# First feed-forward of a hybrid decoder layer: state-space tables built in smaller steps, modulation sums held in their place, fewer table stores

## The chip, the cores and the metric

The kernel runs on one core of a Trainium2 chip. The metric is the device time of one execution in microseconds (us); a run of the kernel before takes 1685.62 us (median of three, 1685.13 to 1685.9). The engines are named as in the profile: PE multiplies matrices (PEld loads its weights), DVE is the vector engine, ACT the scalar engine, POOL is GpSimd, and SP is the engine whose queue issues most of the transfers (DMA).

## The reference, cut to what matters

One decoder layer on a 1024 x 1024 activation, all in 32-bit floats: a gated feed-forward, a mixer of a short convolution and a diagonal state-space model (S5), a second gated feed-forward, a final norm. Shift, scale and gate of each part come from the condition vector.

```python
mod = c_act @ w_mod[l] + b_mod[l]                 # 9 vectors of 1024
h = modulate(rms_norm(x, ffn1_norm[l]), sh1, sc1)
x = x + 0.5 * g1 * swiglu(h, w_gate, w_up, w_down)        # first feed-forward
h = modulate(rms_norm(x, mix_norm[l]), sh2, sc2)
proj = h @ w_in[l]
...
lam_bar = jnp.exp(lam * dt)                       # per group (32) and state (64)
b_bar = ((lam_bar - 1) / lam)[..., None] * b
bu = jnp.einsum('gpc,bsgc->bsgp', b_bar, u)
_, states = lax.associative_scan(combine, (lam_bar, bu), axis=1)
y = jnp.einsum('gcp,bsgp->bsgc', c, states).real + d_skip * u
...
x = x + 0.5 * g3 * swiglu(h2, w_gate, w_up, w_down)       # second feed-forward
```

## The kernel before, in words

Every large product is made of 128 x 512 tiles from operands that are split in a high and a low part; three matmuls (high by high, high by low, low by high) make one product, which the text calls a triple (`mm3`). After each triple a counter (`Clock.tick`) advances, and after every `period` triples one step of a side program (`clock.side`) is recorded. So work for other engines is laid between the matmuls in units of triples. A scheduler then orders each engine's instructions by when their inputs should be there, so an instruction may stand in its engine's queue well before the place at which it was recorded, unless `V.follow` ties it behind another one.

The first feed-forward is `fa0` to `fa10`, eleven groups of 256 hidden columns, and then `fad` and `fald`, its down projection. Groups 1 to 10 use a product with seven multiplications instead of eight (`seven`): seven weight tiles `w`, each for a gate (`g`) and an up (`u`) half of four triples, added up in the PSUM banks A, B and C, in the order B, C, B, C, B, A, B. DVE reads the second C, the third B, the A and the last B and adds them to copies that ACT took earlier (`fa5gu`, `fa5gc`, `fa5gt` and so on). Each weight tile comes as a `raw` tile by DMA; ACT rounds it to the high part, DVE subtracts it to get the low part (both rows are called `w<-raw`), and between two uses of one raw tile POOL starts a DMA that adds another block to it. Four `w` tiles and three raw tiles exist. Sums of the results go to DRAM (`kept`).

Beside the groups a side program (`side1`) works off three things: the left factors of the seven products, then the base of the state-space tables (`ssm_base`), and then eight batches (`ssm_batch`), one for each four of the 32 state groups, with the 24 modulation sums between them.

A batch loads its parameters `prm`, and DVE makes `bb` (the scaled input matrix), `cl` (an output table, with `clt` as its second term), `bl` (an input table, with `blt`) and the rotors `rot` and `rott`. PE then makes `kp` (the kernel of the short Toeplitz matrix) and `tp` (`bl` transposed). ACT copies these to `kc` and `mi`, DVE adds the skip term to the diagonal of `kc`, and the tables go to DRAM: `mo_d`, `co_d`, `si_d`, `mi_d` and the Toeplitz matrices `mk_d`. These rows share four buffers (`bt`). The mixer loads the tables again later.

A modulation sum (`wm`) is one DVE instruction over a 128 x 1024 weight block that a DMA of 512 KB fetches into one of two buffers; the fetch after it waits until the sum has freed the buffer. Before the change, one sum stands after the input table and three after the PE work of each of batches 2 to 7, and nothing ties them to that place.

The line numbers are of little help, since one helper (L113) records nearly every instruction; the rows are found by the names of their tiles.

Of the kernel before, what the change touches and what calls it, by code (L numbers as in the profile page):

```python
# [21 lines left out]
P = 128  # L22
# [9 lines left out]
CH = 16  # L32
# [199 lines left out]
def hymba_layer(ctx: ExitStack, tc, x_d, xt_d, wm1_d, wmod_d, gu1_d, gs1_d, ds10_d, ds11_d, wl1_d, win_d, wout_d, glu_d, gu2_d, gs2_d, wd2_d, ds20_d, ds21_d, ds22_d, wl2_d, cols_d, cond_d, lam_d, bc_d, out_d):  # L232
# [775 lines left out]

    cact_d = scratch.tile([P, 1024], F32, name="cact_d")
    SP.dma_start(cact_d[:], cact[:])  # L1010
    mk_d = scratch.tile([NB, P, GB * P], F32, name="mk_d")
    mi_d = scratch.tile([NB, P, GB * P], F32, name="mi_d")
    mo_d = scratch.tile([NB, P, GB * P], F32, name="mo_d")
    co_d = scratch.tile([NB, P, GB * P], F32, name="co_d")
# [25 lines left out]
    def ssm_base(sb, sb1):  # L1040
# [127 lines left out]
            yield  # L1168
        zero = sb1.tile([CH, 112], F32, name="zero")
        V.memset(zero[:], 0.0)  # L1170
        mk4 = mk_d[:].rearrange("b p (g c) -> p b g c", g=GB)
        for t in range(1, TAU):
            for b in range(NB):
                SP.dma_start(
                    mk4[t * CH : (t + 1) * CH, b, :, 0 : t * CH],
                    zero[:, 0 : t * CH].unsqueeze(1).to_broadcast([CH, GB, t * CH]),
                )
            yield
        ssm.update(q=qq, tabs=tabs, base=baset, step=step, lam=lam)

    def ssm_batch(b):
        bp = bps[0]
        gs = slice(b * GB, (b + 1) * GB)
        prm = bp.tile([P, 4, GB, CH], F32, tag="prm", name=f"prm{b}")
        SP.dma_start(prm[:], bc_d[b])
        bb = bp.tile([P, 2, GB, CH], F32, tag="bb", name=f"bb{b}")
        q = tuple(ssm["q"][:, i, gs].unsqueeze(2).to_broadcast([P, GB, CH]) for i in range(2))
        cmul(bp, bb[:], prm[:, 0:2], q, [GB, CH], f"bb{b}")
        p1, p2, e1, e2 = ssm["tabs"]

        def bt(name):
            return bp.tile([P, 576], F32, tag="bt", name=name, bufs=4)

        def comb(dst, n, lam, src, op, nm):

            t = bt(nm)[:, : GB * n * CH].rearrange("p (g n c) -> p g n c", g=GB, n=n)
            la = [a[:, 0:n, gs].rearrange("p n g -> p g n").unsqueeze(3).to_broadcast([P, GB, n, CH]) for a in lam]
            sc = [a.unsqueeze(2).to_broadcast([P, GB, n, CH]) for a in src]
            V.tensor_tensor(out=dst, in0=la[0], in1=sc[0], op=ALU.mult)
            V.tensor_tensor(out=t, in0=la[1], in1=sc[1], op=ALU.mult)  # L1200
            yield
            V.tensor_tensor(out=dst, in0=dst, in1=t, op=op)

        cl = bt(f"cl{b}")
        cl4 = cl[:].rearrange("p (g n c) -> p g n c", g=GB, n=9)
        yield from comb(cl4, 9, (p1, p2), (prm[:, 2], prm[:, 3]), ALU.add, f"clt{b}")
        SP.dma_start(mo_d[b].rearrange("p (g m) -> p g m", g=GB), cl4[:, :, 1:9, :].rearrange("p g n c -> p g (n c)"))
        bl = bt(f"bl{b}")
        bl4 = bl[:, :512].rearrange("p (g n c) -> p g n c", g=GB, n=8)
        yield from comb(bl4, 8, (e1, e2), (bb[:, 0], bb[:, 1]), ALU.add, f"blt{b}")  # L1210
        if b >= 2:
            yield from gate1()

        def v3(a):
            return a[:, :512].rearrange("p (g m i) -> p g m i", g=GB, m=8)

        bs = [a[:, gs, :].unsqueeze(2).to_broadcast([P, GB, 8, 16]) for a in ssm["base"]]
        st = [ssm["step"][:, i, :, gs].rearrange("p m g -> p g m").unsqueeze(3).to_broadcast([P, GB, 8, 16]) for i in range(2)]

        def rotors():  # L1220

            r, t = bt(f"rot{b}"), bt(f"rott{b}")
            V.tensor_tensor(out=v3(r), in0=st[0], in1=bs[0], op=ALU.mult)
            V.tensor_tensor(out=v3(t), in0=st[1], in1=bs[1], op=ALU.mult)
            yield
            V.tensor_tensor(out=r[:, :512], in0=r[:, :512], in1=t[:, :512], op=ALU.add)
            A.activation(t[64:128, :512], r[64:128, :512], AF.Copy, scale=-1.0)
            for half in (slice(0, 64), slice(64, 128)):
                SP.dma_start(co_d[b, half], r[0:64, :512])
            SP.dma_start(si_d[b, 0:64], r[64:128, :512])  # L1230
            SP.dma_start(si_d[b, 64:128], t[64:128, :512])

        yield from rotors()
        yield

        kp = sm([CH, 512], f"kp{b}")
        for g in range(GB):
            T.matmul(
                kp[:, g * P : (g + 1) * P], lhsT=bl4[:, g, 7, :], rhs=cl4[:, g, 0:8, :].rearrange("p n c -> p (n c)"), start=True, stop=True
            )  # L1240
        tp = sm([P, 512], f"tp{b}")
        for g in range(GB):
            T.transpose(tp[:, g * P : (g + 1) * P], bl[:, g * P : (g + 1) * P], ident[:])
        if b >= 2:
            yield from gate1()
            yield from gate1()
            yield from gate1()
        kc = bt(f"kc{b}")
        kc3 = kc[:CH, :512].rearrange("p (g m) -> p g m", g=GB)
        A.copy(kc[:CH, :512], kp[:])  # L1250
        for g in range(GB):
# [3 lines left out]
        mk3 = mk_d[b].rearrange("p (g m) -> p g m", g=GB)  # L1255
        for t in range(TAU):
            SP.dma_start(mk3[t * CH : (t + 1) * CH, :, t * CH :], kc3[:, :, : P - t * CH])
        mi = bt(f"mi{b}")
        A.copy(mi[:, :512], tp[:])
# [39 lines left out]
    def side1():  # L1299
        yield from combos1()  # L1300
        clock.period = 4.5
        sb = side_open.enter_context(tc.tile_pool(name="sb", bufs=1, side="right"))
        with tc.tile_pool(name="sb1", bufs=1, side="right") as sb1:
            yield from ssm_base(sb, sb1)
        clock.period = BATCH_PERIOD
        bps.append(side_open.enter_context(tc.tile_pool(name="bp", bufs=1, side="right")))
        mod_home.pool = side_open.enter_context(tc.tile_pool(name="wmp", bufs=1, side="right"))
        share[0] = MODS[1]
        for _ in range(2):
            mod_fetch(mod_home)  # L1310
        for b in range(NB):
            yield from ssm_batch(b)

    def side2(home, n):

# [16 lines left out]
            norm_into(act2, h, n2[h], 1, "h2")  # L1332

    movs["B"] = es1.enter_context(tc.tile_pool(name="movB1", bufs=12))
    BATCH_PERIOD = 5.5
    first_open = ExitStack()

    def first_opened():
# [528 lines left out]
```

## Time and profile before

| | us |
|---|---|
| median of three runs | 1685.62 |
| the profiled execution | 1691.33 |
| its span, first to last instruction | 1689.6 |
| PE busy | 1656.7 |
| DVE busy | 1080.9 |
| ACT busy | 685.9 |

The profiled execution is one run with the profiler on, and 5.7 us longer than the median; 1.7 us of its time lie outside the span. PE is busy in nearly all of it. A PE that is busy is not one at its full rate: a row of 12 matmuls that follows another one starts 2.72 us after it at the full rate, and whatever makes this distance longer is lost time.

### The profile page before, as it was taken

The numbers are of one execution on the slowest core, as the hardware profiler recorded it, in microseconds if no ns is written. First come the engines' busy times: TensorE is split into PE (matmuls) and PEld (weight loads), VectorE is DVE, ScalarE is ACT, GpSimd is POOL, SyncE is SP. The second block draws the span as 40 slices with busy tenths as digits, with TensorE's granted clock in tenths as the row PEclk, the third lists the DMA queues.
The fourth block names the chain that finished last, engine by engine and source line by source line (L and its number), as shares of the span: only waits on it lengthen the run. The fifth ranks groups of instructions, "written<-read, shape, count | busy, mean of one in ns | idle before, by whom it ended". The sixth has DMA issues, their size and how long they took to land.

```text
span 1689.6 us, 20672 instructions
## 1 busy us (share of the span) xinstructions
PE 1656.7 (98%) x7509; PEld 1364.8 (81%) x7509; DVE 1080.9 (64%) x1608; ACT 685.9 (41%) x1011; POOL 173.4 (10%) x211
## 2 busy tenths in 40 slices
PE   8999989999999999999999999999999999999998
PEld 5888878878888888787878778888888888888887
DVE  7984777777567758635656847856555555344576
ACT  6654333343465431332214416434444444322345
POOL 2010000001001102100000121001000111000104
PEclk9999999999999999999999999999999999999999
DMA  9467987987898767145653333557887777889832
GB/s 350 138 162 183 264 250 205 266 250 208 256 317 230 181 213 273 38 112 161 200 152 117 97 103 138 137 137 215 228 239 216 211 224 225 271 276 314 245 77 100
DMA packets 128840, 337.06 MB, mean 199 GB/s; under 512 B 22369, under 2 KB 37985, under 8 KB 127714
## 3 DMA queue, kind: packets, MB, share of 16 engines
q1 hardware_dynamic: 112034, 275.96, 47.2%
q0 software_dynamic: 16704, 59.78, 20.3%
q8 instruction: 59, 0.97, 0.2%
q14 instruction: 43, 0.35, 0.1%
HBM read 253.37 MB, written 73.92 MB: 194 GB/s over the span
## 4 chain that ended last, share of the span: by engine, by line
PE 73%; DVE 7%; DMA 5%; issue 1%; SPq 1%; ACT 0%; POOL 0%; DVEq 0%; POOLq 0%; ACTq 0%
PE fald L113 4%; PE wo L113 3%; PE fbd_1B L113 3%; PE fbd_0B L113 3%; PE fad_0B L113 3%; PE fad_1B L113 3%; PE b L113 2%; PE c L113 2%; PE u L113 2%; PE v L113 2%; DMA wm<-in_wmod 2%; PE fbd_1C L113 1%; PE fbd_0C L113 1%; PE fb0u L113 1%; PE fb0d L113 1%
## 5 line engine op out<-in xcount | busy, mean ns | idle before, releaser
L113 DVE TENSOR_TENSOR w<-raw,w 128x1024 fp32r<-128x1024 f32 (+1 forms) x247 | 298.7, 1211 | 264.3 <-ACT w L113 259.9
L113 ACT CAST w<-raw 128x1024 fp32r<-128x1024 f32 (+1 forms) x247 | 256.2, 1039 | 310.5 <-DMA raw<-in_ds 75.6
L175 POOL DMA_DIRECT2D raw<-in_gs x80 | 70.6, 883 | 740.5 <-DVE w L113 461.7
L113 DVE CUSTOM_DVE_ANT_0 wm<-wm,cact 128x1024 f32<-128x1024 f32 x56 | 76.1, 1373 | 36.3 <-DMA wm<-in_wmod 36.1
L175 POOL DMA_DIRECT2D raw<-in_ds x36 | 31.5, 876 | 311.9 <-DVE w L113 177.6
L113 PE MATMUL p<-h,w 128*128 128x512 f32 x192 | 48.7, 401 | 2.3 <-ACT h L113 1.5
L113 PE MATMUL wo<-oa,w 128*128 128x512 f32 x192 | 47.0, 400 | 2.7 <-ACT w L113 2.6
L113 PE MATMUL wo<-ob,w 128*128 128x512 f32 x192 | 45.6, 392 | 1.1 <-ACT ob L113 0.6
L113 PE MATMUL c<-h,w 128*128 128x512 f32 x192 | 46.1, 393 | 0.0
L113 PE MATMUL v<-h,w 128*128 128x512 f32 x192 | 46.0, 393 | 0.0
L113 PEld LDWEIGHTS wo<-oa,w 128*128 128x128 f32 x192 | 36.7, 193 | 11.4 <-ACT w L113 3.0
L113 PE MATMUL u<-h,w 128*128 128x512 f32 x192 | 45.5, 396 | 0.2 <-DVE h L113 0.2
L113 PE MATMUL b<-h,w 128*128 128x512 f32 x192 | 45.1, 392 | 0.0
L113 PEld LDWEIGHTS p<-h,w 128*128 128x128 f32 x192 | 35.1, 189 | 10.6 <-ACT h L113 2.0
L113 PEld LDWEIGHTS wo<-ob,w 128*128 128x128 f32 x192 | 35.7, 188 | 9.2 <-ACT ob L113 1.0
L113 PEld LDWEIGHTS u<-h,w 128*128 128x128 f32 x192 | 36.2, 190 | 8.3 <-DVE h L113 0.6
L113 PEld LDWEIGHTS b<-h,w 128*128 128x128 f32 x192 | 35.7, 188 | 7.2
L113 PEld LDWEIGHTS c<-h,w 128*128 128x128 f32 x192 | 35.7, 189 | 7.0
L113 PEld LDWEIGHTS v<-h,w 128*128 128x128 f32 x192 | 35.5, 188 | 7.0
L113 DVE TENSOR_TENSOR X<-co,X 128x512 f32<-128x512 f32 x8 | 5.5, 693 | 36.1 <-DMA swx<-X 28.1
L113 PE MATMUL fb0u<-h,w 128*128 128x512 f32 x96 | 23.8, 391 | 0.0
L113 PE MATMUL fb0g<-h,w 128*128 128x512 f32 x96 | 23.2, 389 | 0.0
(1554 smaller groups left out, 3882.9 us busy)
## 6 DMA issues: line engine op xcount, KB each, us to landing
raw<-in_gs SPq DMA_DIRECT2D x80, 512.0 KB, 4.8
raw<-in_gs POOLq DMA_DIRECT2D x80, 512.0 KB, 6.5
wm<-in_wmod SPq DMA_DIRECT2D x56, 512.0 KB, 7.2
raw<-in_ds SPq DMA_DIRECT2D x32, 512.0 KB, 5.8
raw<-in_ds POOLq DMA_DIRECT2D x32, 512.0 KB, 7.5
mw<-in_wm SPq DMA_DIRECT2D x8, 1024.0 KB, 8.3
raw<-in_win SPq DMA_DIRECT2D x16, 512.0 KB, 4.4
xb<-in_xt SPq DMA_DIRECT2D x8, 512.0 KB, 9.4
```

The lines of the kernel that those rows point to most:

```text
L113: r = getattr(self.engine, name)(*args, **kw)
L175: self.G.dma_start(out=r, in_=src, accum_op=ALU.add)
```

## The change

Five things are changed in the batches and around them.

- The steps are finer: a batch is cut into 13 pieces instead of five, and one step is recorded every 2.3 triples instead of every 5.5.
- After pieces 1, 5 and 9 of every batch one modulation sum is recorded (three to a batch, 24 in all, as before), and `pools["mixed"] = False` makes each sum follow the DVE instruction that was recorded just ahead of it.
- `kp` and `tp` come after the rotors' last addition; the rotors' copy and stores come behind them.
- The parameters of a batch are loaded during the batch before it.
- A Toeplitz row in DRAM has 256 columns, of which the last 128 take what sticks out, so that one store writes all eight shifted copies of a group's kernel: four stores to a batch instead of eight, and seven stores of zeros instead of 56. The mixer's load of `mk` then reads four rows of 512 bytes in a partition instead of one of 2 KB.

```diff
-    mk_d = scratch.tile([NB, P, GB * P], F32, name="mk_d")
+    mk_row = NB * GB * 2 * P
+    mk_all = scratch.tile([P * mk_row + P], F32, name="mk_d")
+    mk_d = mk_all[: P * mk_row].rearrange("(p b g m) -> b p g m", p=P, b=NB, g=GB)[:, :, :, :P]
+    mk_steps = mk_all[:].rearrange("(t r) -> t r", t=TAU)[:, : CH * mk_row].rearrange("t (c b g m) -> b c t g m", c=CH, b=NB, g=GB)[:, :, :, :, :P]
...
         for t in range(1, TAU):
-            for b in range(NB):
-                SP.dma_start(
-                    mk4[t * CH : (t + 1) * CH, b, :, 0 : t * CH],
...
+            SP.dma_start(
+                mk4[t * CH : (t + 1) * CH, :, 0 : t * CH],
...
     def ssm_batch(b):
...
-        prm = bp.tile([P, 4, GB, CH], F32, tag="prm", name=f"prm{b}")
-        SP.dma_start(prm[:], bc_d[b])
+        prm = ssm["prm"]
...
+        if b + 1 < NB:
+            prm_load(b + 1)
...
-        if b >= 2:
-            yield from gate1()
...
-        if b >= 2:
-            yield from gate1()
-            yield from gate1()
-            yield from gate1()
+        A.activation(t[64:128, :512], r[64:128, :512], AF.Copy, scale=-1.0)
...
-        for t in range(TAU):
-            SP.dma_start(mk3[t * CH : (t + 1) * CH, :, t * CH :], kc3[:, :, : P - t * CH])
...
+        for g in range(GB):
+            SP.dma_start(mk_steps[b][:, :, g, :], kc3[:, g, :].unsqueeze(1).to_broadcast([CH, TAU, P]))
...
+        prm_load(0)
         for _ in range(2):
             mod_fetch(mod_home)
+        yield
+        pools["mixed"] = False
         for b in range(NB):
-            yield from ssm_batch(b)
+            for i, _ in enumerate(ssm_batch(b)):
+                yield
+                if i % 4 == 1:
+                    yield from gate1()
...
-    BATCH_PERIOD = 5.5
+    BATCH_PERIOD = 2.3
```

DVE's queue around the start of `fa4`'s second C and of the first weight tiles of `fa5`, before (the row `ISA wm` is a sum, the short row `ISA gate` or `ISA scl` reads its result):

```order
L113 TENSOR_TENSOR w_1788<-raw_1641,w_1788 128x1024
L113 ISA wm_2_1_2408,gate<-wm_2_1_2408,cact 128x1024
L113 ISA gate 128x1
L113 ISA wm_3_0_2545,gate<-wm_3_0_2545,cact 128x1024
L113 ISA gate 128x1
L113 TENSOR_TENSOR w_1854<-raw_1474,w_1854 128x1024
L113 ISA wm_3_1_2638,gate<-wm_3_1_2638,cact 128x1024
L113 ISA gate 128x1
L113 TENSOR_TENSOR fa4gu_1814<-fa4gu_1814,fa4gC 128x512
L113 TENSOR_TENSOR gate<-gate,cols 128x8
L113 ISA wm_0_0_2659,scl<-wm_0_0_2659,cact 128x1024
```

And the same place of it now:

```order
L113 TENSOR_TENSOR w_1746<-raw_1634,w_1746 128x1024
L113 TENSOR_TENSOR w_1801<-raw_1474,w_1801 128x1024
L113 TENSOR_TENSOR fa4gu_1765<-fa4gu_1765,fa4gC 128x512
L113 ISA wm_0_0_1782,gate<-wm_0_0_1782,cact 128x1024
L113 ISA gate 128x1
L113 TENSOR_TENSOR fa4uu_1799<-fa4uu_1799,fa4uC 128x512
L113 SCALAR_TENSOR_TENSOR fa4Y<-fa4uu_1799,fa4gu_1765 128x512
L113 TENSOR_TENSOR w_1842<-raw_1713,w_1842 128x1024
```

Before, nine sums stand ahead of or among these rows; now three do, and from here to `w_1926`, the tile of `fa5`'s first C, there is none.

SP's queue at the end of `fa4`, before:

```order
L113 DMA raw_1857<-in_gs 128x1024
L113 DMA wm_0_1_2693<-in_wmod 128x1024
L113 DMA wm_1_0_2836<-in_wmod 128x1024
L113 DMA wm_1_1_2925<-in_wmod 128x1024
L113 DMA wm_2_0_2956<-in_wmod 128x1024
L113 DMA wm_2_1_2977<-in_wmod 128x1024
L113 DMA mk_d<-kc_1965 16x512
L113 DMA mk_d<-kc_1965 64x1x112
L113 DMA mk_d<-kc_1965 64x1x96
```

And now:

```order
L113 DMA raw_1804<-in_gs 128x1024
L113 DMA wm_2_0_1945<-in_wmod 128x1024
L113 DMA kept4X<-fa4X 128x1024
L113 DMA raw_1929<-in_gs 128x1024
L113 DMA mk_d<-kc_1976 16x8x128 x2
L113 DMA kept4Y<-fa4Y 128x1024
L113 DMA kept4Z<-fa4Z 128x1024
L113 DMA mk_d<-kc_1976 16x8x128
L113 DMA kept4W<-fa4W 128x1024
```

Five fetches in a row, each waiting for a sum, have become single ones with weight loads and stores between them.

DVE's queue from the second batch's input table to the first addition that PE's second `kp` of the program stands behind, now:

```order
L113 TENSOR_TENSOR w_2083<-raw_1929,w_2083 128x1024
L113 ISA wm_2_0_1945,gate<-wm_2_0_1945,cact 128x1024
L113 ISA gate 128x1
L113 TENSOR_TENSOR bl_2095<-bl_2095,blt_2096 128x512
L113 TENSOR_TENSOR rot_2139<-rs,rt_1405 128x512
L113 TENSOR_TENSOR rott_2140<-rs,rt_1406 128x512
L113 TENSOR_TENSOR rot_2139<-rot_2139,rott_2140 128x512
L113 TENSOR_TENSOR w_2128<-raw_1749,w_2128 128x1024
L113 TENSOR_TENSOR fa5gu_2108<-fa5gu_2108,fa5gC 128x512
```

On PE this `kp` now stands in the third B of `fa5`, behind the second C that the last row reads; before, it stood in the first C of `fa5`, and on DVE the end of `bl` came after `fa4Z`.

## Rows read from the trace of the kernel before

**Rows 1.** The page's first part: busy time, share of the span, instructions.

```profile
PE 1656.7 (98%) x7509; PEld 1364.8 (81%) x7509; DVE 1080.9 (64%) x1608; ACT 685.9 (41%) x1011; POOL 173.4 (10%) x211
```

**Rows 2.** Stretches: length, busy PE, PEld, DVE, ACT, POOL (instructions), PE's clock, DMA share, GB/s.

```profile
230.00:270.00 40.00, 35.00 (x160) 28.04 (x159) 31.92 (x58) 13.32 (x20) 2.66 (x3) 1.00 0.82 242
350.00:390.00 40.00, 38.81 (x176) 31.41 (x175) 33.49 (x59) 15.94 (x22) 4.43 (x5) 1.00 0.87 220
390.00:430.00 40.00, 40.00 (x183) 32.81 (x183) 27.00 (x42) 15.47 (x21) 3.62 (x5) 1.00 0.77 205
```

**Rows 3.** PE in order of time: start, length, engine, instruction.

```profile
190.41 2.88 PE L113 MATMUL fa4gB<-h,w 128*128 128x512 f32 x12
193.13 2.88 PE L113 MATMUL fa4uB<-h,w 128*128 128x512 f32 x12
...
266.98 2.88 PE L113 MATMUL fa5uA<-h,w 128*128 128x512 f32 x12
...
274.00 2.88 PE L113 MATMUL fa5uB<-h,w 128*128 128x512 f32 x12
...
358.56 2.88 PE L113 MATMUL fa8gB<-h,w 128*128 128x512 f32 x12
```

**Rows 4.** Waits of PE from 60 to 480 us: total, times, longest.

```profile
PE kp L113 <- DVE bl L113: 3.3, 1, 3.3
PE fa5gC L113 <- DVE w L113: 1.7, 1, 1.7
PE fa7gB L113 <- DVE fa7gc L113: 1.2, 1, 1.2
PE fa6gB L113 <- DVE fa6gc L113: 0.5, 1, 0.5
```

**Rows 5.** In order of time, 230 to 246 us, with idle time before and its releaser.

```profile
231.14 1.23 DVE L113 CUSTOM_DVE_ANT_0 wm<-wm,cact 128x1024 f32<-128x1024 f32 x1 [1.98 <-DMA wm<-in_wmod]
...
233.28 1.21 DVE L113 CUSTOM_DVE_ANT_0 wm<-wm,cact 128x1024 f32<-128x1024 f32 x1
...
236.57 1.21 DVE L113 TENSOR_TENSOR w<-raw,w 128x1024 fp32r<-128x1024 f32 x1
...
237.83 2.56 PE L113 MATMUL fa5gC<-h1S,w 128*128 128x512 f32 x10 [1.68 <-DVE w L113]
...
244.93 0.67 DVE L113 TENSOR_TENSOR bl<-bl,blt 128x512 f32<-128x512 f32 x1
...
245.75 1.03 PE L113 MATMUL kp<-cl,bl 128*16 128x128 f32 x8 [3.32 <-DVE bl L113]
```

**Rows 6.** DVE's groups by shape, 190 to 440 us: busy, mean ns, idle before.

```profile
L113 DVE TENSOR_TENSOR w<-raw,w 128x1024 fp32r<-128x1024 f32 x44 | 53.7, 1220 | 24.8 <-ACT w L113 24.7
L113 DVE CUSTOM_DVE_ANT_0 wm<-wm,cact 128x1024 f32<-128x1024 f32 x21 | 25.6, 1220 | 18.9 <-DMA wm<-in_wmod 18.8
L113 DVE TENSOR_TENSOR cl<-tab,prm 128x576 f32<-128x576 f32 x7 | 5.3, 755 | 0.4 <-issue 0.3
...
L113 DVE TENSOR_TENSOR blt<-tab,bb 128x512 f32<-128x512 f32 x7 | 4.8, 684 | 4.3 <-DMA mk_d<-kc 4.3
...
L113 DVE SCALAR_TENSOR_TENSOR kc<-ident,lam,kc 16x16 f32<-16x16 f32 x28 | 4.6, 217 | 2.0 <-ACT kc L113 2.0
```

**Rows 7.** The tile `wm`, 160 to 360 us: its fetches from issue to landing.

```profile
DMA to landing us min/median/max: 3.9/6.7/9.8
```

**Rows 8.** SP's queue in order of time, 205 to 250 us: start, length, transfers.

```profile
215.48 17.25 SPq L113 DMA_DIRECT2D wm<-in_wmod  x5
...
233.21 4.82 SPq L113 DMA_DIRECT2D mk_d<-kc  x8
```

**Rows 9.** Transfers by line: count, KB each, median us from issue to landing.

```profile
mk<-mk_d SPq DMA_DIRECT2D x8, 256.0 KB, 4.0
...
ub<-u_d SPq DMA_DIRECT2D x8, 256.0 KB, 4.9
```

**Rows 10.** Waits of PE in the mixer, 690 to 1080 us.

```profile
PE yy L113 <- DVE co L113: 4.3, 3, 2.6
```

More of the change, by code (lines that the diff above doesn't have):

```diff
@@ L1170, in ssm_base, with prm_load @@
         V.memset(zero[:], 0.0)
-        mk4 = mk_d[:].rearrange("b p (g c) -> p b g c", g=GB)
+        mk4 = mk_all[: P * mk_row].rearrange("(p q m) -> p q m", p=P, q=NB * GB)
         for t in range(1, TAU):
-            for b in range(NB):
-                SP.dma_start(
-                    mk4[t * CH : (t + 1) * CH, b, :, 0 : t * CH],
-                    zero[:, 0 : t * CH].unsqueeze(1).to_broadcast([CH, GB, t * CH]),
-                )
+            SP.dma_start(
+                mk4[t * CH : (t + 1) * CH, :, 0 : t * CH],
+                zero[:, 0 : t * CH].unsqueeze(1).to_broadcast([CH, NB * GB, t * CH]),
+            )
             yield
         ssm.update(q=qq, tabs=tabs, base=baset, step=step, lam=lam)
+    def prm_load(b):
+        ssm["prm"] = bps[0].tile([P, 4, GB, CH], F32, tag="prm", name=f"prm{b}")
+        SP.dma_start(ssm["prm"][:], bc_d[b])
     def ssm_batch(b):
@@ L1202, in comb @@
             V.tensor_tensor(out=dst, in0=dst, in1=t, op=op)
+            yield
         cl = bt(f"cl{b}")
@@ L1218, in ssm_batch @@
         st = [ssm["step"][:, i, :, gs].rearrange("p m g -> p g m").unsqueeze(3).to_broadcast([P, GB, 8, 16]) for i in range(2)]
[L1220 to L1233, printed above, removed]
+        r, t = bt(f"rot{b}"), bt(f"rott{b}")
+        V.tensor_tensor(out=v3(r), in0=st[0], in1=bs[0], op=ALU.mult)
+        yield
+        V.tensor_tensor(out=v3(t), in0=st[1], in1=bs[1], op=ALU.mult)
+        yield
+        V.tensor_tensor(out=r[:, :512], in0=r[:, :512], in1=t[:, :512], op=ALU.add)
         yield
@@ L1243, in ssm_batch @@
             T.transpose(tp[:, g * P : (g + 1) * P], bl[:, g * P : (g + 1) * P], ident[:])
-        if b >= 2:
-            yield from gate1()
-            yield from gate1()
-            yield from gate1()
+        A.activation(t[64:128, :512], r[64:128, :512], AF.Copy, scale=-1.0)
+        for half in (slice(0, 64), slice(64, 128)):
+            SP.dma_start(co_d[b, half], r[0:64, :512])
+        SP.dma_start(si_d[b, 0:64], r[64:128, :512])
+        SP.dma_start(si_d[b, 64:128], t[64:128, :512])
+        yield
         kc = bt(f"kc{b}")
@@ L1250, in ssm_batch @@
         A.copy(kc[:CH, :512], kp[:])
+        mi = bt(f"mi{b}")
+        A.copy(mi[:, :512], tp[:])
+        yield
         for g in range(GB):
@@ L1254, in ssm_batch @@
             )
-        mk3 = mk_d[b].rearrange("p (g m) -> p g m", g=GB)
-        for t in range(TAU):
-            SP.dma_start(mk3[t * CH : (t + 1) * CH, :, t * CH :], kc3[:, :, : P - t * CH])
-        mi = bt(f"mi{b}")
-        A.copy(mi[:, :512], tp[:])
+        for g in range(GB):
+            SP.dma_start(mk_steps[b][:, :, g, :], kc3[:, g, :].unsqueeze(1).to_broadcast([CH, TAU, P]))
         SP.dma_start(mi_d[b], mi[:, :512])
@@ L1308, in side1 @@
         share[0] = MODS[1]
+        prm_load(0)
         for _ in range(2):
             mod_fetch(mod_home)
+        yield
+        pools["mixed"] = False
         for b in range(NB):
-            yield from ssm_batch(b)
+            for i, _ in enumerate(ssm_batch(b)):
+                yield
+                if i % 4 == 1:
+                    yield from gate1()
     def side2(home, n):
```

## The prediction

> **What bounds the kernel now.** I read the page first. PE is busy in 98% of the span [rows 1], so only its rate and its gaps can move the end. Then I read busy time by stretches of 40 us, to see where PE is idle beside the batches. From 230 to 270 us it lacks 5.0 us, from 350 to 390 us it lacks 1.2 us, and in the stretch behind that nothing, although the last two batches still run there [rows 2]. The granted clock stands at 1.00 in all of them, so the lost time is idle time and not a slower array.
>
> Busy time hides small delays, so I count the program's rows instead. A half tile of 12 matmuls starts 2.72 us after the one before it (190.41 to 193.13). One `kp` with its `tp` costs 1.58 us: from 266.98 to 274.00 lie two half tiles and one such pair, 7.02 - 5.44. From the start of `fa4` to that of `fa8` are 168.15 us [rows 3]. Four groups of 14 half tiles make 152.32 us, and the five pairs in them (at 220, 246, 270, 306 and 341 us) 7.90 us. So **7.9 us are lost** there. Four waits are named between 60 and 480 us, 6.7 us together [rows 4]; the other 1.2 us are delays that lie inside matmuls just behind them.
>
> All four waits end with a DVE row, so the next view is DVE's queue ahead of such a row. At 231 us DVE stands idle for 1.98 us, until the block of a modulation sum has landed, does that sum (1.23 us) and soon another (1.21 us), and comes to the low part of a weight tile only at 236.57, for which PE waits 1.68 us. A further sum stands behind it, and the end of `bl` comes at 244.93; PE waits 3.32 us for that [rows 5]. So 4.4 us of sums and their waits stand ahead of the first wait, 5.6 us ahead of the second, more than PE lost at either. Over the whole part DVE stood idle for 18.9 us ahead of sums [rows 6]. Why the blocks come late is seen on SP: one piece of its queue holds five fetches and lasts 17.25 us [rows 8]. Each waits for a buffer that the sum two before it frees, and then takes 6.7 us to land (3.9 to 9.8) [rows 7]. The sums were pulled far ahead of the batches that they were written in: as the order shows, nine stand up to the end of `fa4`, where three will now.
>
> **The change part by part.** *Held sums.* A batch is 13 steps and three sums, 16 steps of 2.3 triples, 36.8 triples of 0.68 us (a quarter of 2.72), so 25.0 us, and 26.6 us with its PE pair. The sums lie 8.9 us apart on average, and with two buffers a fetch is asked for some 17 us before its use, against a landing of at most 9.8 us [rows 7]. Most of the 18.9 us of idle DVE should go. They are not even, though: a sum follows the DVE row recorded just ahead of it, and where that row is a table's and is pulled forward, the sum goes along. The order shows two places that are tight. Near 170 us the second and third sum use one buffer with some 4 us of DVE work between them, so DVE may wait up to 5.8 us. Behind `fa5W` a buffer is freed about 7 us of work before its next sum, a wait of up to 2.8 us.
>
> What DVE may be late without a loss follows from PE's order. The third B must be read before the last B writes into the same bank, and three half tiles lie between, 8.16 us; less the addition itself (0.68 us, as a `blt` row) about **7.5 us**. Both places stay under it. For `fa5`, the two weight tiles that PE takes first have no sum between `fa4gu` and them, and `bl` of the second batch now ends before the second C is read, with `kp` behind that C. I put the gain of this part at the whole 7.9 us; its lower end is nothing.
>
> *Finer steps.* The table work is not less, only denser: a batch's DVE rows are four `bb` (about 1.0 us), three like `cl` (755 ns), six like `blt` (684) and four `kc` (217), 8.2 us, and three sums 3.7 us, so 11.9 us in 26.6. A group of the feed-forward has seven low parts (1220 ns) and 14 additions and joins of about 0.69 us, 18.2 us in the 39.7 us of a group with its share of pairs [rows 6]. That is 45% and 46%; since a row starts about 0.08 us before the one ahead has ended, the true load is some 83%. From 350 to 390 us DVE was 84% busy (33.49 of 40 us), with no sum in it, and PE lost only the wait that the sums before had left [rows 2]. So such a load is borne if nothing blocks the queue. For new small waits I take 1.0 us, twice the smallest of rows 4. The ends are 0 and the 1.7 us of the middle wait in each of the eight batches, 13.6 us.
>
> *Fewer stores.* 64 Toeplitz stores become 32, and 56 zero stores seven. Eight of them hold SP for 4.82 us [rows 8], so 81 fewer free some 49 us of that queue. DVE waited 4.3 us for such stores before a `blt` [rows 6], and four stores free its buffer about 2.4 us sooner. No PE wait ends there now, so I take 0; what could be won at most is inside the 7.9 us. The cover is the 8 us above; without it a late `bl` would cost PE its full delay. The prefetched parameters and the later copy of the rotors on ACT come under the same answer: off the path, 0.
>
> *The mixer's loads.* `mk` is read in pieces of 512 bytes instead of 2 KB. The nearest row is `ub`, as many bytes in pieces of 512: 4.9 us against 4.0 us for `mk` now [rows 9]. So 0.9 us more in each of eight loads, 0 to 7.2 us. PE's waits in the mixer are for `co` [rows 10], a chain of other transfers on the same queue, which a longer load can delay; `mk` itself is asked for a batch early. I take 0.3 us.
>
> The Trainium skill, in "DMA: Bandwidth & Descriptors", section "Bandwidth" (Why small descriptors are slow), speaks against this part: each packet has a fixed overhead of about three cycles on top of one for 32 bytes. By that, 512 bytes cost 19 cycles for 16 and 2 KB 67 for 64, an estimate of 13% more, 0.5 us a load and 4.2 us for eight if all were on the path, against 7.2 us by the rows.
>
> *Sum.* -7.9 + 1.0 + 0.3 = **-6.6 us**. The profiled execution would go from 1691.33 to 1684.7 us. It is 5.7 us longer than the median; if the profiler's share of that lay in these very waits, a plain run would win only 0.9 us. I see no sign that it does, and take the whole: 1685.6 - 6.6 = **1679.0 us**.
>
> **The rivals.** What a measurement here can tell from no change is about 0.2%, 3.4 us.
>
> *The lateness is not the sums'.* DVE also stood idle for 24.7 us ahead of low parts, until ACT had rounded a tile whose block came late [rows 6]; this chain stays. And the holding is weaker than its name says, as above. If half the waits come back elsewhere, or a plain run has fewer of them, 0 to 3.4 us are won: about 1684 us.
>
> *DVE falls behind, slower.* The place is the third B of each group, where the denser tables, a sum and the additions meet. If DVE is more than 7.5 us late there, PE waits in every batch. It decides from 1.0 us a batch on (8 x 1.0 us eat up the 7.9); at the middle wait of 1.7 us it is 13.6 + 0.3 - 7.9 = 6.0 us slower, 1691.6 us. For it speaks the load of 83%, against it the stretch with 84%.
>
> *The mixer pays.* If all eight loads delay the chain of `co`, 7.2 us come back: -7.9 + 1.0 + 7.2 = +0.3, 1685.9 us. Against it: only three waits of `yy` are seen, 4.3 us in all [rows 10].
>
> **How the numbers follow.** My forecast has a chance of 0.62, with a range of its own of 1677.5 to 1681.6 us (from all of the 7.9 us with nothing new, to 4 us won). The lateness that stays has 0.20, DVE falling behind 0.11, the mixer 0.07. Faster by over 0.2% is the forecast and 0.03 of the first rival, 0.65. Slower is 0.01, 0.10 and 0.03 of the three, 0.14. The rest, 0.21, lies within 0.2%. The range reaches from 1676.5, a little past all of the lost time, to 1687.0 us, which holds the first and the third rival and leaves out most of the second, about 0.1, and little below.
>
> **What would show it.** In the new profile `fa4` to `fa8` should take 160.5 to 162 us with as many pairs, DVE's idle time ahead of sums should fall from 18.9 to under 6 us, no piece of SP's queue should hold several fetches for more than 10 us, and the waits of PE between 60 and 480 us should add up to 2 us at most. The forecast is wrong if PE waits for `fa5gc` or its like in several groups, for `kp` again, or if `yy` waits longer than 4.3 us.

## The result, and the profile after

The changed kernel takes 1690.89 us (median of 20 runs, 1686.29 to 1700.25), the kernel before beside it 1685.97 us (20 runs, 1684.03 to 1690.27). The ratio is 1.0025, 95% interval 1.0017 to 1.0034: about 4.9 us slower, where 6.6 us less were predicted. The profiled execution took 1687.72 us, one of the shorter ones of the changed kernel; that of before was longer than all 20 of its runs. So the two profiles are compared stretch by stretch and not by their sums.

The page's first line, against [rows 1]: PE's work has not changed.

```profile
PE 1654.5 (98%) x7509; PEld 1362.0 (81%) x7509; DVE 1083.2 (64%) x1608; ACT 684.6 (41%) x1011; POOL 174.1 (10%) x211
```

Stretches after the change, in the columns of [rows 2], with two more from the end of the first feed-forward:

```profile
230.00:270.00 40.00, 40.00 (x183) 32.82 (x182) 31.66 (x51) 14.24 (x20) 3.53 (x4) 1.00 0.81 220
350.00:390.00 40.00, 39.81 (x185) 32.00 (x184) 32.57 (x56) 13.98 (x20) 3.55 (x4) 1.00 0.88 251
390.00:430.00 40.00, 40.00 (x184) 32.88 (x184) 31.98 (x56) 15.91 (x23) 3.53 (x4) 1.00 0.94 259
430.00:470.00 40.00, 39.09 (x171) 31.75 (x170) 20.10 (x26) 18.53 (x29) 3.53 (x4) 1.00 0.96 312
470.00:505.00 35.00, 30.91 (x132) 24.05 (x131) 27.09 (x37) 22.04 (x35) 2.63 (x3) 1.00 0.86 273
```

The 5.0 us that PE lacked from 230 to 270 us are gone, and 4.1 us are missing from 470 to 505, a stretch in which it lacked nothing before (35.00 of 35.00).

Starts on PE, against [rows 3]:

```profile
189.88 2.88 PE L113 MATMUL fa4gB<-h,w 128*128 128x512 f32 x12
...
352.03 1.30 PE L113 MATMUL fa8gB<-h,w 128*128 128x512 f32 x5
...
433.40 2.88 PE L113 MATMUL fa10gB<-h,w 128*128 128x512 f32 x12
...
505.64 0.62 PE L113 MATMUL fad_0A<-fa1lA,w 128*128 128x512 f32 x2
```

From `fa4` to `fa8` are 162.15 us instead of 168.15, with five `kp` pairs again: 1.9 us lost instead of 7.9. The same count can be carried on to the start of `fad_0A`, the A product in the first pass of the down projection. From `fa4` to `fa10` the ideal is six groups of 38.08 us (14 half tiles) and eight pairs of 1.58; from `fa10` to `fad_0A` it is 24 half tiles, 65.28 us. By that PE loses 2.4 us up to `fa10` (before 7.8) and 7.0 us behind it (before 0.1).

Waits of PE from 60 to 480 us and from 480 to 700 us, against [rows 4]:

```profile
PE fa7uB L113 <- DVE fa7uc L113: 1.6, 1, 1.6
PE fa10uB L113 <- DVE fa10uc L113: 1.2, 1, 1.2
PE fa10gC L113 <- ACT fa10gc L113: 0.6, 1, 0.6
...
PE fad_1C L113 <- ACT fad_1c L113: 2.9, 1, 2.9
```

The four waits of before have gone; the new ones are for additions and copies of `fa7`, `fa10` and `fad`. What holds the addition up in `fa7` is seen in order of time (start, length, engine; in brackets idle time before and its releaser), against [rows 5]:

```profile
335.26 0.91 SPq L113 DMA_DIRECT2D si_d<-rot  x1
336.26 0.55 SPq L113 DMA_DIRECT2D si_d<-rott  x1
337.30 5.18 SPq L113 DMA_DIRECT2D mk_d<-kc  x4
337.64 0.67 DVE L113 TENSOR_TENSOR fa7gc<-fa7gc,fa7gB 128x512 f32<-128x512 f32 x1
346.17 0.49 DVE L113 TENSOR_TENSOR bb<-prm,qq 128x128 f32<-128x128 f32 x2 [7.86 <-DMA si_d<-rott]
...
348.44 0.68 DVE L113 TENSOR_TENSOR fa7uc<-fa7uc,fa7uB 128x512 f32<-128x512 f32 x1
349.17 3.02 PE L113 MATMUL fa7uB<-h,w 128*128 128x512 f32 x12 [1.59 <-DVE fa7uc L113]
```

`bb`, the first row of the next batch, stands ahead of the addition `fa7uc` in DVE's queue. Its two intermediate products take buffers of the same ring of four (`tag="bt"`, in the helper `cmul`) in which the rotors `rot` and `rott` still wait to be stored. The last stores of `rot` and `rott` left SP at 335.26 and 336.26 us and landed 10.7 and 10.1 us later; `bb` ran from 346.17 us on. DVE stood idle for 7.86 us with an addition behind it that PE needed.

DVE's groups from 190 to 440 us, against [rows 6]:

```profile
L113 DVE CUSTOM_DVE_ANT_0 wm<-wm,cact 128x1024 f32<-128x1024 f32 x22 | 26.8, 1218 | 0.0
...
L113 DVE TENSOR_TENSOR blt<-tab,bb 128x512 f32<-128x512 f32 x7 | 4.8, 686 | 5.9 <-DMA mk_d<-kc 3.4 <-issue 2.5
...
L113 DVE TENSOR_TENSOR bb<-prm,qq 128x128 f32<-128x128 f32 x14 | 3.8, 286 | 24.4 <-DMA si_d<-rott 9.2 <-DMA mk_d<-kc 5.9 <-DMA wm<-in_wmod 5.8
```

And `bb` in the same view before the change, a row that the groups ahead of the prediction leave out:

```profile
L113 DVE TENSOR_TENSOR bb<-prm,qq 128x128 f32<-128x128 f32 x14 | 3.7, 282 | 6.0 <-PE kp L113 3.2 <-DMA si_d<-rot 2.6
```

The idle time ahead of sums fell from 18.9 us to nothing; 18.4 us came ahead of `bb` instead. The view puts 11.7 of the 24.4 us down to a Toeplitz store and to a sum's fetch. In both places a rotor store landed just ahead of `bb`: issued at 369.68 us, landed after 5.8, `bb` at 375.59; issued at 282.40, landed after 7.0, `bb` at 289.52. So these waits, too, are put down to the rotors here. In the two waits of `blt` a Toeplitz store landed in the same way (320.38 + 5.4 us, `blt` at 325.88; 235.72 + 5.8 us, `blt` at 241.59). The sums' fetches land as before ([rows 7]: median 6.7 us, now 5.7), and SP's longest piece with several of them lasts 4.0 us instead of 17.25 [rows 8].

At the end of the first feed-forward, the first casts of left factors on ACT, and one of them before the change:

```profile
431.55 0.90 SPq L113 DMA_DIRECT2D x<-in_x  x2
...
433.84 0.60 SPq L113 DMA_DIRECT2D x<-in_x  x1
...
435.05 0.49 SPq L113 DMA_DIRECT2D x<-in_x  x1
435.58 0.58 SPq L113 DMA_DIRECT2D fa1lA<-kept1X  x1
...
448.64 0.62 ACT L113 CAST fa1lA<-fa1lA 128x512 fp32r<-128x512 f32 x1 [8.07 <-DMA fa1lA<-kept1X]
...
449.81 0.58 ACT L113 COPY fa10gc<-fa10gC 128x512 f32<-128x512 f32 x1
```

```profile
435.72 0.41 SPq L113 DMA_DIRECT2D fa1lA<-kept1X  x1
...
440.42 0.62 ACT L113 CAST fa1lA<-fa1lA 128x512 fp32r<-128x512 f32 x1 [0.20 <-DMA fa1lA<-kept1X]
```

`fa1lA` was cast 13.1 us after its issue instead of 4.7, since four loads of `x` (512 KB each) now leave SP just ahead of it (without them, in the run after_nox below, it landed in 5.0 us instead of 13.0); ACT stood idle for it, and the copy that PE's next product needs stood behind the cast. In `fad` the casts of `fa5lA` to `fa8lA` do the same to the copy `fad_1c`.

The mixer is as before, against [rows 9] and [rows 10] (transfers with median landing time; waits of PE):

```profile
mk<-mk_d SPq DMA_DIRECT2D x8, 256.0 KB, 3.8
...
ub<-u_d SPq DMA_DIRECT2D x8, 256.0 KB, 3.6
```

```profile
PE yy L113 <- DVE co L113: 4.3, 3, 2.9
```

### The profile page after: what moved, and what is told of

The parts are those of the page before. It is cut to its first block, busy times and chain, and to the rows that moved or that the text cites. A ratio compares the mean times of both kernels' runs of the same rounds, so it can differ in the third digit from the quotient of the medians.

```text
span 1686.0 us, 20578 instructions
## 1 busy us (share of the span) xinstructions
PE 1654.5 (98%) x7509; PEld 1362.0 (81%) x7509; DVE 1083.2 (64%) x1608; ACT 684.6 (41%) x1011; POOL 174.1 (10%) x211
## 4 chain that ended last, share of the span: by engine, by line
PE 60%; DVE 9%; DMA 8%; issue 1%; ACT 1%; SPq 1%; POOL 0%; DVEq 0%; POOLq 0%; ACTq 0%
PE fald L113 4%; PE fbd_0B L113 3%; PE fbd_1B L113 3%; PE fad_1B L113 2%; PE fad_0B L113 2%; PE wo L113 2%; PE u L113 2%; DVE w L113 2%; PE b L113 2%; PE c L113 1%; DMA swx<-X 1%; PE fbd_1C L113 1%; PE fbd_0C L113 1%; PE v L113 1%; PE fb0d L113 1%
## 5 line engine op out<-in xcount | busy, mean ns | idle before, releaser
L113 DVE TENSOR_TENSOR bb<-prm,qq 128x128 f32<-128x128 f32 x16 | 4.3, 286 | 30.5 <-DMA si_d<-rott 9.2
```

The lines of the kernel that those rows point to most:

```text
L113: r = getattr(self.engine, name)(*args, **kw)
```

## The experiments

"Lost" is the count of above, from each run's profiled execution: "early" from `fa4` to `fa10`, "late" from `fa10` to `fad_0A`. Times are medians beside runs of the kernel before on the same chip; runs of one call have the same number in the last column. The late count holds waits and, in some runs, a clock that fell behind a wait; both are taken apart below.

| kernel | lost early, late | us | before | ratio (95%) | call |
|---|---|---|---|---|---|
| before | 7.8, 0.1 | | | | |
| changed kernel | 2.4, 7.0 | 1690.89 | 1685.97 | 1.0025 (1.0017 to 1.0034) | |
| before_again | 7.2, 0.8 | 1688.77 (one) | 1688.23 | | 1 |
| after_again | 5.5, 7.7 | 1692.02 (one) | 1688.23 | | 1 |
| slow_pace | 0.0, 5.4 | 1687.54 | 1688.23 | 0.9998 (0.9986 to 1.001) | 1 |
| x_late | 0.2, 7.5 | 1695.82 | 1688.23 | 1.004 (1.0027 to 1.0053) | 1 |
| pace_25 | 2.9, 7.8 | 1692.86 | 1688.28 | 1.0027 (1.0016 to 1.0039) | 2 |
| no_hold_25 | 14.7, 0.2 | 1695.93 | 1688.28 | 1.0043 (1.0028 to 1.0057) | 2 |
| stores_only | 13.1, 0.7 | 1694.46 | 1688.28 | 1.0042 (1.0026 to 1.0057) | 2 |
| hold_only | 1.3, 8.0 | 1692.06 | 1688.28 | 1.0022 (1.0009 to 1.0036) | 2 |
| after_nox | 3.9, 2.9 | 1685.24 | 1688.38 | 0.998 (0.9968 to 0.9991) | 3 |
| before_nox | 9.1, 0.1 | 1686.89 | 1688.38 | 0.9988 (0.9976 to 1.0) | 3 |
| x_in_fad_26 | 0.0, 0.6 | 1683.64 | 1688.38 | 0.997 (0.9957 to 0.9984) | 3 |
| old_stores | 0.0, 6.2 | 1685.59 | 1688.38 | 0.9977 (0.9964 to 0.9989) | 3 |
| sums_last | 0.0, 1.5 | 1681.26 | 1688.16 | 0.9962 (0.9949 to 0.9975) | 4 |
| rot_early | 0.8, 9.7 | 1687.68 | 1688.16 | 0.9992 (0.9977 to 1.0007) | 4 |
| after_third | 4.0, 8.3 | 1695.05 | 1688.16 | 1.0042 (1.0026 to 1.0058) | 4 |
| old_stores_x_in_fad | 1.0, 1.6 | 1686.92 | 1688.16 | 0.9999 (0.9988 to 1.001) | 4 |
| sums_last_again | 0.0, 0.7 | 1681.12 | 1686.89 | 0.9964 (0.9951 to 0.9976) | 5 |
| sums_last_old | 0.0, 4.0 | 1683.87 | 1686.89 | 0.9983 (0.9972 to 0.9995) | 5 |

### Both kernels once more, and where the loss lies

**before_again** and **after_again** have no edit.

> The kernel before, unchanged, profiled once more. Theory A (what the change wins in the first feed-forward is real, and it is given back where the down projection begins): PE again loses 6 to 8 us between the starts of fa4 and fa8 and under 0.5 us between fa8 and the third B of the down projection. Rival B (the profiled execution that was shown was an unusual one, the lost time is not in a plain run): at most 3 us are lost between fa4 and fa8.

> The changed kernel, unchanged, profiled once more. Theory A: fa4 to fa8 loses about 2 us as in the first profile, and 6 to 12 us are lost in fa10 and in the first pass of fad, behind casts of left factors whose blocks land late. Rival C (the mixer reads the Toeplitz tables in small pieces and pays): nothing of note is lost in fa10 and fad, and yy, px and b lose 4 us more than before.

Waits of PE in before_again (60 to 480 us), and in after_again:

```profile
PE kp L113 <- DVE bl L113: 3.3, 1, 3.3
PE fa5gC L113 <- DVE w L113: 1.7, 1, 1.7
```

```profile
PE fa7uB L113 <- DVE fa7uc L113: 3.2, 1, 3.2
PE fa10uB L113 <- DVE fa10uc L113: 1.7, 1, 1.7
PE fa8gB L113 <- DVE fa8gc L113: 1.2, 1, 1.2
```

The letters name the explanations that the expectations set against each other. Rival B falls: the two largest waits of [rows 4] are there again to a tenth of a microsecond, in an execution of 1688.77 us, so the time that the prediction counted as lost is lost in ordinary runs. Rival C falls, since neither the waits for `co` nor `mk` grew. In after_again, 13.2 us are lost against 7.9 before; the difference of 5.3 us is about the measured loss of 4.9.

### Pace and the place of the loads of x

**slow_pace** changes one number (**pace_25** makes it 2.5), **x_late** moves the call that loads `x` behind the fetches of `fa1lA` to `fa4lA` (of its longer lines only the argument that changes is shown, here and below):

```diff
-    BATCH_PERIOD = 2.3
+    BATCH_PERIOD = 2.6
...
             open_x(ctx)
-            load_x(range(2), (0, 2))
...
-    then=(lambda left: fetch_chunk(0, left))
+    then=(lambda left: (fetch_chunk(0, left), load_x(range(2), (0, 2)) if left == "A11" else None))
```

> The changed kernel with one step every 2.6 triples instead of 2.3, so that the last batch ends at fa10 as before and the loads of x and of the left factors keep their old place. Theory A: the waits in fa10 and fad go, those between fa4 and fa8 stay small, and the time is 1679 to 1682 us, 4 to 7 us under the kernel before. Rival B: 1685 to 1687 us. Rival C: as the changed kernel, 1690 to 1692 us.

> The changed kernel with the four loads of x recorded behind the fetches of the first four left factors, so that these no longer queue behind 1.5 MB of x. Theory A: the casts of fa1lA wait 2 us instead of 8, the waits in fa10 fall by 2 to 3 us, that of fad_1C stays since the casts of fa5lA to fa8lA still stand ahead of its copy; 1686 to 1689 us. Rivals B and C: as the changed kernel, 1690 to 1692 us.

> The changed kernel with one step every 2.5 triples, the one pace at which the transfers and ACT's rows behind fa9 stand almost as in the kernel before (fa1lA and fa2lA fetched ahead of x, no cast of fa5lA ahead of the copies of fad). Theory A (won between fa4 and fa8, lost again by the order of fetches and casts in fa10 and fad): fa4 to fa8 loses under 2 us, fa10 and the first pass of fad under 1 us, and the time is 5 to 7 us under the kernel before, 0.996 to 0.997 of it. Rival D (the region from fa10 on is bound by transfers whatever the order, since the tables' stores have grown to 64 KB each): 4 to 5 us are still lost in fad, and the time is that of the kernel before.

Theory A missed in all three. slow_pace loses nothing up to `fa10` (the idle time ahead of `bb` is 3.2 us there), so the early part of theory A holds, but 5.4 us are lost in `fad`. In pace_25 the transfers stand in the same order as before the change (`fa1lA` and `fa2lA`, the Toeplitz stores, `fa3lA`, the loads of `x`, `fa4lA`), and 7.8 us are lost all the same. So the order of the queues, theory A's narrow form, is not the cause. Its largest wait, the stretch behind `fa10` in the kernel before, and two stretches of pace_25:

```profile
PE fad_0C L113 <- DVE fa10gt L113: 4.7, 1, 4.7
```

```profile
460.00:485.00 25.00, 25.00 (x112) 20.70 (x111) 20.73 (x31) 16.76 (x28) 2.65 (x3) 1.00 1.05 330
```

```profile
475.00:485.00 10.00, 5.29 (x23) 4.06 (x21) 8.02 (x14) 7.15 (x14) 0.53 (x1) 0.86 1.05 353
485.00:490.00 5.00, 4.55 (x13) 3.19 (x12) 5.00 (x8) 5.00 (x10) 0.00 (x0) 0.59 0.80 236
```

The DMA share stands at 1.05 in both kernels; PE of pace_25 reaches `fa10` 3.6 us sooner, and what it needs next does not come sooner (the cast of `fa4lS` that ACT has ahead of it ran at 482.30 us, before at 478.72). That leaves rival D, a stretch that transfers limit, with a larger loss than its 4 to 5 us.

Not all of the late loss is waiting. Behind the wait of 4.7 us the granted clock fell, to 0.59 on average from 485 to 490 us, and triples followed each other in 1.28 us instead of 0.68 until about 489 us. In hold_only it stood at 0.50 from 485 to 490 us, the lower of its two levels (1.2 instead of 2.4 GHz), behind a wait of 3.2 us; in slow_pace and old_stores it fell behind one of 3.3 us. From the distances of the triples, the clock took by estimate 1.6 to 2.9 us of the late loss in each of these four runs. In the first two profiles of the changed kernel it stayed at 1.00; in the third it was 0.70 from 500 to 505 us.

In x_late the scheduler still sent two of the loads ahead of the left factors, at 428.11 us. Its median lies 9 us above its own profiled execution (1686.44 us), which is also its shortest run. That run had a mean granted clock of 0.995, the seven runs above 1695 us one of 0.991 or 0.993; where in the kernel it was lower was not seen.

### The parts one by one

**no_hold_25** is pace_25 without `pools["mixed"] = False`. **hold_only** puts that line ahead of the batches of the kernel before, **stores_only** the new Toeplitz layout into the kernel before. **old_stores** is the changed kernel with the old layout:

```diff
-        for g in range(GB):
-            SP.dma_start(mk_steps[b][:, :, g, :], kc3[:, g, :].unsqueeze(1).to_broadcast([CH, TAU, P]))
+        for t in range(TAU):
+            SP.dma_start(mk3[t * CH : (t + 1) * CH, :, t * CH :], kc3[:, :, : P - t * CH])
```

> As the run with 2.5 triples, but without the line that makes each sum follow the DVE row recorded ahead of it; the end of the first feed-forward has the same order. If holding the sums is what wins (the prediction's step), sums are again pulled ahead, PE loses 4 to 8 us between fa4 and fa8, and the time is 4 to 7 us above the other. If the finer pieces win by themselves, the two are equal.

> The kernel before with the line that holds the sums alone; they stay in the coarse steps, three in a row behind the PE work of a batch. The last batch's stores and with them the fetches of x and of the left factors come later than before. Theory A: fa4 to fa8 loses under 3 us instead of 7.9, and fad loses what late left factors cost, 3 us or more; so about the time of the kernel before. If the hold does nothing, 7 to 8 us are lost between fa4 and fa8.

> The kernel before with the new Toeplitz layout alone (four stores to a batch, seven stores of zeros, mk read in pieces of 512 bytes). Theory A: the mixer and what follows take as long as before, the time is within 2 us of the kernel before unless the order at fa10 moves. Rival C (the mixer pays): 3 to 7 us slower, lost from px to b.

> The changed kernel with the old Toeplitz layout (eight stores to a batch, 56 stores of zeros, mk read in pieces of 2 KB); all else of the change stays. With the sums held, the layout should matter little: as the changed kernel within 2 us. If the 64 KB stores (256 KB to a batch instead of 144) fill the transfer engines, it is 2 to 5 us faster; if the many stores hold up the queue of SP, it is slower.

Waits of PE from 60 to 510 us in no_hold_25, in hold_only and in stores_only:

```profile
PE fa4gB L113 <- DVE fa4gc L113: 4.5, 1, 4.5
PE fa4gC L113 <- DVE w L113: 2.9, 2, 1.6
PE fa5gC L113 <- DVE w L113: 1.7, 1, 1.7
```

```profile
PE fad_0B L113 <- ACT fad_0t L113: 3.2, 1, 3.2
```

```profile
PE fa4gB L113 <- DVE fa4gc L113: 5.9, 1, 5.9
```

Holding the sums does what the prediction said of it: the kernel before goes from 7.8 to 1.3 us lost early by that line alone, and without it the fine pieces lose 14.7. In time, though, pace_25 is only 3.1 us under no_hold_25, with intervals that overlap, since it loses 7.8 us late and no_hold_25 0.2. And hold_only hands 8.0 us back in `fad` (and 2.6 us more behind it). The layout alone makes the kernel before 0.42% slower, and not in the mixer: with 81 stores fewer on SP the sums are pulled still further ahead (17 of them done by 240 us, 14 in the kernel before), DVE stands idle for 21.7 us ahead of them (190 to 440 us), and PE loses 13.1 us. In the changed kernel the old layout is worth 8 us (0.9977 against 1.0025 in the first comparison), against the 2 us that were expected: the early loss goes, with `blt` waiting 0.7 us instead of 5.9 and `bb` 19.6 instead of 24.4.

### Is it the transfers

**after_nox** and **before_nox** take 4 MB out of the stretch, and with them the residual out of the result; GpSimd writes zeros instead:

```diff
+    def zero_x(hs, ks):
...
+                nc.gpsimd.memset(xt[k][h][:], 0.0)
...
-            load_x(range(2), (0, 2))
+            zero_x(range(2), (0, 2))
```

**x_in_fad_26** is slow_pace with the first four loads recorded inside `fad`:

```diff
-            load_x(range(2), (0, 2))
...
-    lambda left: load_x(range(2), (1, 3)) if left == "A12" else None
+    lambda left: load_x(range(2), dict(A11=(0, 2), A12=(1, 3)).get(left, ()))
```

> The changed kernel without the eight loads of x (4 MB) at the end of the first feed-forward: GpSimd fills these tiles with zeros instead, so the residual is left out. The casts of left factors still stand ahead of copies on ACT, nearly as in the changed kernel. Theory E (what PE wins earlier it waits for again since the stretch from fa10 through the first pass of fad is bound by transfers, not by the order of the queues): the loss in fa10 and the first pass of fad falls from 7 to 8 us to under 2, and the time is 5 to 7 us under that of the changed kernel, 1682 to 1686 us. Theory A in its narrow form (the order on ACT): half of the loss or more stays.

> The kernel before without the eight loads of x, in the same way. Theory E: it loses only 0.1 to 0.7 us there, so nothing is won by it, 1685 to 1688 us, within 0.2% of the kernel before, and the loss of 7 to 8 us between fa4 and fa8 stays. If loads of x cost something of their own beside the order (the clock, the later parts), it gets faster as well.

> The changed kernel with one step every 2.6 triples and the first four loads of x recorded inside the first pass of fad, where they are queued behind nearly all left factors. Theory E: left factors land sooner, PE loses under 3 us in fad instead of 5.3 at the same pace, and the time is 3 to 6 us under the kernel before unless x itself comes late. Theory A: the copies stand ahead of the late casts, same result. If neither holds, 1687 to 1690 us.

Without `x` the changed kernel loses 2.9 us late instead of 7.0 to 8.3, and takes 0.998 of the kernel before instead of 1.0025; the late waits for ACT's copies in `fad` stay, 2.3 us of them. The kernel before, with nothing to win late, gains 0.12%, an interval that just reaches 1. x_in_fad_26 sends the left factors first (`fa1lA` to `fa4lA` at 441 to 442 us, `x` from 468 us on) and loses 0.6 us late, 2.1 us in the second pass of `fad` where `x` itself is late, and is 0.3% faster than the kernel before.

### The wait of bb

**sums_last** moves two of a batch's sums behind its last two pieces, so that five steps instead of three lie between the rotors' stores and the next `bb`:

```diff
-                if i % 4 == 1:
+                if i in (5, 11, 12):
                     yield from gate1()
```

> The changed kernel with the same pace and the same number of steps, but two of a batch's three sums stand between its last piece and the bb of the next batch, so that bb needs its table buffers some 3 us of steps later. Theory F (bb waits for the stores of the rotors, 24 to 28 us of idle DVE, and the additions of a group are queued behind it): the idle time ahead of bb falls below 18 us, the loss of PE in fa7 and fa8 falls from 2.4 to 5 us to under 1, and the time is 2 to 4 us under the changed kernel of the same call; fa10 and fad keep their 6 to 8 us. Theory G (fa7 and fa8 lose by the plain load of DVE): no change.

**rot_early** records the rotors' copy and stores behind their last addition, ahead of `kp`, which makes the steps up to the next `bb` five as well:

```diff
         V.tensor_tensor(out=r[:, :512], in0=r[:, :512], in1=t[:, :512], op=ALU.add)
+        A.activation(t[64:128, :512], r[64:128, :512], AF.Copy, scale=-1.0)
+        for half in (slice(0, 64), slice(64, 128)):
+            SP.dma_start(co_d[b, half], r[0:64, :512])
...
         yield
```

> The changed kernel with the rotors' copy and stores ahead of kp and tp again, as before the change; the order from fa9 on is the same. Theory F: the buffers of the rotors come free sooner, the idle time ahead of bb falls, and with it the loss in fa7 and fa8, by 1 to 3 us. But the scheduler then puts bb still further ahead among the additions, so that it may be nothing. If the place of these stores doesn't matter: as the changed kernel within 1 us.

**after_third** is the changed kernel again, **old_stores_x_in_fad** joins what its name says, at one step every 2.6 triples.

> The changed kernel, unchanged, beside the others of this call: 1.002 to 1.004 of the kernel before, 9 to 13 us lost from fa4 through the first pass of fad.

> All that won so far: held sums and fine pieces at one step every 2.6 triples, the first loads of x inside fad, and the old Toeplitz layout. Theories E and F: PE loses 3 us at most from fa4 through fad, and the time is 5 to 8 us under the kernel before, 0.995 to 0.997 of it. If the layout and the order at fad remove the same loss, it is as the run with x inside fad, 0.997.

In sums_last: DVE's `bb` from 190 to 440 us; two stretches; SP's last Toeplitz stores and first loads of `x`.

```profile
L113 DVE TENSOR_TENSOR bb<-prm,qq 128x128 f32<-128x128 f32 x14 | 3.7, 284 | 11.4 <-DMA si_d<-rot 8.9 <-ACT kc L113 1.6 <-DMA si_d<-rott 0.9
```

```profile
230.00:270.00 40.00, 40.00 (x183) 32.78 (x183) 32.63 (x54) 15.14 (x21) 3.53 (x4) 1.00 0.94 269
...
430.00:470.00 40.00, 40.00 (x178) 33.14 (x177) 23.39 (x32) 21.61 (x34) 3.52 (x4) 1.00 1.03 340
```

```profile
412.68 2.68 SPq L113 DMA_DIRECT2D mk_d<-kc  x4
...
420.81 1.41 SPq L113 DMA_DIRECT2D x<-in_x  x3
```

Theory F holds, and more than it said followed. The idle time ahead of `bb` fell from 24.4 us to 11.4 (13.7 in sums_last_again), the loss in `fa7` and `fa8` to nothing, and the late loss too, to 1.5 us. With DVE no longer stopped, sums and tables are done sooner and more is transferred early on (a DMA share of 0.94 from 230 to 270 us instead of 0.81); the last batch's Toeplitz stores leave from 412.68 us on instead of 422.19, and the first loads of `x`, whose tiles open when the side program's are closed, at 420.81 instead of 431.55, 12 us ahead of the first left factor instead of 4. The kernel takes 1681.26 us, 14 us under the changed kernel of the same call, where 2 to 4 were expected, and 0.38% under the kernel before. rot_early reaches half of it: `bb` waits 19.9 us and the early loss is 0.8 us, but 9.7 us are lost late. old_stores_x_in_fad is slower than either of the two that it joins. Its profiled execution (1683.38 us, its shortest) loses 2.6 us up to `fad_0A`, and 2.3 us more in the second pass of `fad`, as x_in_fad_26 does.

PE does not pay for the sum of DVE's idle time, though. x_late and old_stores have 21.6 and 19.6 us of it ahead of `bb` and lose 0.2 and 0.0 us early. What PE pays for is the one wait with `fa7uc` behind it: 7.86, 8.12 and 7.71 us long in the three profiles of the changed kernel, for 1.6, 3.2 and 2.4 us of PE; 5.33 us (and 0.98 a little later) in x_late and 2.24 us in old_stores, for nothing. That fits the 7.5 us by which the prediction let DVE be late.

> The kernel with two sums behind each batch's last piece, unchanged, once more. If its gain is real: 0.995 to 0.998 of the kernel before, at most 3 us lost from fa4 through the first pass of fad.

> The same with the old Toeplitz layout. With the original places of the sums, the old layout ran at 0.9977 and the new at 1.0025 to 1.0042 of the kernel before. If the layout cost time only since bb and the additions waited for table buffers, it makes no difference here, within 2 us of the other. If the 64 KB stores cost time by themselves, it is 4 to 8 us faster.

**sums_last_old** is sums_last with old_stores' layout. The gain holds (0.9964), and here the old layout is no faster (0.9983, some 3 us slower). So, as far as this pair shows, the layout cost time only through waits that sums_last has taken away.

## Why the prediction was wrong

- *What bounds the kernel.* Right up to `fa10`: 7.2 and 9.1 us are lost early in two more profiles of the kernel before or nearly it, and holding the sums takes most of it away (hold_only 1.3). The term "-7.9", taken with the new early waits, measured -5.4 us in the changed kernel's first profile and -2.4 and -3.9 in the next two.
- *The step that failed.* "The prefetched parameters and the later copy of the rotors on ACT come under the same answer: off the path, 0." The rotors' stores leave later, and the next batch needs their buffers three steps of 2.3 triples behind them, where five steps of 5.5 had lain between in batches 2 to 7: 24.4 to 27.7 us of idle DVE ahead of `bb`, 2.4 to 5.5 us of PE. I counted DVE's rows and not the ring of four buffers that they go through. sums_last, with five steps again, brought the early loss to 0.0 in both of its profiles. "What could be won at most is inside the 7.9 us" failed with it, since the new stores could also cost time: the 64 KB stores took 4.6 us to land (1.9 to 9.3), against 3.2 us for the smaller ones before, and `blt` waited 5.9 us for them (4.3 before).
- *The step that was missing.* The sum ended at `fa8`. The tables' end sets when `x` is loaded, and PE's own gain brings it to `fa10` sooner: every kernel that reached `fa10` by 437.0 us with the loads of `x` among the left factors lost 5.4 to 9.7 us behind it, with `x` sent earlier, later or not at all 0.6 to 4.0; those that came after 437.5 lost 0.1 to 0.8. These two limits only sort the runs; that transfers bind there is shown by the runs that moved `x` or left it out. None of the four waits of [rows 4] is left in the changed kernel, so that in place of the term "1.0" for new small waits stand 9.4 to 13.2 us from `fa4` on, more than the 7.9 us won.
- *Its signs.* Idle time ahead of sums under 6 us and no long piece of fetches came true. `fa4` to `fa8` was 162.15 us, just past the 160.5 to 162; the waits up to 480 us were 3.9 us instead of 2. One sign that it named against itself came, too: PE waited for `fa7uc` and its like in `fa7`, `fa8` and `fa10`.
- *The rivals.* "The lateness is not the sums'" is refuted by hold_only. "DVE falls behind" named the right place, the additions at the end of a group, and 1691.6 us. Its cause, the load, was not it, though the load came out near the forecast 83% (DVE was busy for 32.57 of 40 us from 350 to 390 us): in sums_last DVE bears the same rows without loss up to `fa10`. That its number is near the measured 1690.89 is luck, as more than half of the loss lay behind `fa10`. "The mixer pays" is refuted: `mk` lands in 3.8 us (4.0 before), and `yy` waits 4.3 us as before. By the Trainium skill, "DMA: Bandwidth & Descriptors", section "Bandwidth" (a fixed overhead for each packet), such a load would grow by an estimated 13%, as worked out in the prediction. One pair of profiles can't show that, since `ub`, a load that was not changed, went from 4.9 to 3.6 us between them. But over all 20 profiles of this text the medians of `mk` average 3.9 us with pieces of 512 bytes (13 profiles) and 3.9 us with pieces of 2 KB (seven), so no growth is seen.
- *Open.* Why sums_last loses 4.0 us late with the old layout and 0.7 to 1.5 with the new one; why rot_early, with five steps as well, wins only half as much; where the longer runs of x_late and old_stores_x_in_fad lose their time; and what the early loading of the parameters and the later place of `kp` and `tp` are worth, which no run tested by themselves.

## What to carry to other kernels

When work is packed closer, count the buffers it passes through as well as its instructions: a buffer whose last reader is a store comes free only when the store has landed (here 4.9 to 10.7 us after its issue, at the waits that were looked at), and the first row that needs it stops everything behind it on its engine. Count, too, what stands behind that row: most of the idle time cost nothing here. Follow a gain to the next stretch in which transfers are the limit; there an engine that comes earlier waits longer (hold_only won 6.5 us early and lost 7.9 us more late), unless what it needs is sent earlier too. Of several pieces of work, put those that share no buffer (here the sums) into the gap that the stores need.

## What the runs showed that was not expected

Fewer instructions in one queue made the kernel slower: the layout with 81 stores less on SP, put alone into the kernel before, cost 0.42%, and with it the scheduler let the sums run still further ahead. And the spread of runs differs from kernel to kernel: in the first comparison the kernel before varied by 6.2 us, the changed one by 14.0; x_late by 11.9, sums_last_again by 6.4. In every kernel of the experiments with six runs or more the longer runs had, on the whole, a lower mean granted clock of TensorE. In slow_pace the shortest run, 1681.10 us, had 0.997 and the two longest, 1691.89 and 1692.63 us, 0.990; 0.7% of 1681 us are 11.8 us, about the difference. Since the clock fell behind waits in the profiles above, a wait can cost more than it lasts. What set the clock of the longer runs was not seen.
